# One in five of the low parts of the expert weights is formed on POOL

## The chip, the core and the metric

The kernel runs on one core of a Trainium2 chip. Its time is device microseconds (us) for one execution. Five engines work side by side, each through its own list of instructions in order: PE (TensorE) multiplies matrices, DVE (VectorE) and POOL (GpSimd) do elementwise work, ACT (ScalarE) does copies and functions, SP issues transfers. An instruction that waits for a semaphore holds up what stands behind it on the same engine.

## The reference

The computation is two transformer blocks on 256 tokens of width 1024, everything in fp32. The first has two layers; the second layer ends in a mixture of 8 experts, of which each token uses 2:

```
logits = xt @ router
top_v, top_i = top_k(logits, 2)
gates = one_hot(top_i) * softmax(top_v), summed over the two
out = sum over e of gates[:, e] * ((silu(xt @ w1[e]) * (xt @ w3[e])) @ w2[e])
```

Here w1[e] and w3[e] are 1024 x 1408 and w2[e] is 1408 x 1024. After it the second block (attention of two kinds, then a feed-forward layer) works on the result.

## The kernel before

**Split weights.** A matrix product in fp32 is made of three products in a faster format, fp32r. Each operand is cut in a high part h (the value rounded to fp32r) and a low part l (the value less h). `mm3` issues h·h, h·l and l·h into the same bank of PSUM. So each weight must be cut before PE can use it. The class `Stream` does that for all weights of the kernel, in the order of a list written beforehand (`plan`).

**One piece of weight.** `pump` issues a load from SP into a raw buffer as soon as one is free. A raw buffer holds 2048 elements in each of 128 partitions, which is two pieces of 1024 (or of 768, or in part of 512). `split` takes the next piece: ACT copies it, rounded, into the high tile, and DVE subtracts, `l = raw - h`, into the low tile. Both inputs of the subtraction lie in SBUF. When the last piece of a raw buffer has been cut, the buffer may be loaded again. `take` calls `split` first, so that the cutting of a piece is written out `ahead` pieces before the piece is used.

**Tiles for the parts.** High and low parts lie in a ring of four pairs of tiles (`wh`, `wl`). In the expert stage a fifth pair is there, a fixed tile named `more`, and `ahead` is 3 instead of 2. `turn` counts the pieces modulo five, and the pieces with turn 4 go to `more`. An expert has 36 pieces, all eight have 288, and 57 of these go to `more`.

**The expert stage.** For pairs of experts, the tokens that chose them are gathered by products with a 0/1 matrix (`gathered`, up to 128 tokens for each expert). Then for each expert, in three steps over the hidden width (512, 512 and 384), the products with w1 and w3 are made (`gemm`, tokens stationary), SiLU on ACT and the product of the two on DVE (tile `esil`), a transposition by PE, and a cut of the hidden values (`eh` on ACT, `el` on DVE) in `hidden_task`. The products with w2 follow, in two halves of 512 columns. `scatter_task` cuts the result (`yh`, `yl`), multiplies it by the 0/1 matrix and adds it to the sum with the gate as a factor (DVE, tile `X`). `drive` takes these tasks in turns, by a fixed rate. It reads no times, so the order of the instructions of this stage is fixed by the program alone.

**A second pass.** If more than 128 tokens chose one expert, a branch does the experts again for the rest, with a new `Stream` that has no `more` tile. The trace of before shows one pass.

**The planner's clocks.** Each engine is wrapped in a `Clock`, which adds up an assumed cost for every instruction written out. The stages before and after the experts are put in order by `timed`, which compares these clocks. The assumed cost is 200 + 2.0 ns for each element on POOL, and 160 + 1.04 ns for each element for a subtraction on DVE.

**POOL** does some clearing of tiles at the start, four copies of 128 x 128 in the second layer, and issues transfers. In the expert stage it has nothing to do.

In the trace nearly all instructions have line 47, where the wrapper calls the engine, so they are told apart by their tiles.

Of the kernel before, what the change touches and what calls it, by code (L numbers as in the profile page):

```python
# [153 lines left out]
def tile_net(ctx: ExitStack, tc: tile.TileContext, A, out):  # L154
# [4 lines left out]
    PE, ACT, DVE, POOL, SP = engines  # L159
# [33 lines left out]
    class Res:  # L193
# [3 lines left out]
        def __init__(self, pool, name, n, shape=(128, 512), dtype=F32):  # L197
            self.args = (list(shape), dtype)
            self.pool, self.name, self.n, self.free = pool, name, n, n
# [76 lines left out]
    class Pool:  # L276
# [7 lines left out]
        def give(self):  # L284
            self.free += 1
# [17 lines left out]
    class Stream:  # L303
        def __init__(self, base):
            self.base = base
            self.ahead, self.phase, self.ends = 2, 0, []
            self.more, self.turn = [], 0
            self.plan, self.loaded, self.subs = [], [], []
            self.at_load = self.at_split = self.at_take = 0
            self.limit = 1 << 30  # L310
# [38 lines left out]
        def split(self, ahead):  # L349
            self.pump()  # L350
            while self.at_split <= self.at_take + ahead and self.at_split < len(self.subs):
                v, n, c, give, phase = self.subs[self.at_split]
                if phase > self.phase:
                    return
                self.turn = (self.turn + 1) % (4 + len(self.more))
                if self.turn < 4:
                    h, l = (wsp.tile([128, 1024], F32R, name=x, tag=x) for x in ("wh", "wl"))
                else:
                    h, l = self.more[self.turn - 4]
                h, l = (x[:, :n * c].rearrange("p (k c) -> p k c", c=c) for x in (h, l))  # L360
                ACT.copy(out=h, in_=v)
                DVE.tensor_sub(out=l, in0=v, in1=h)
                self.subs[self.at_split] = (n, h, l)
                if give is not None:
                    give()
                self.at_split += 1
                self.pump()
# [8 lines left out]
    ws = Stream([main_raw])  # L376
# [59 lines left out]
    def drive(main, live, pend, rate=1.0, most=7, bg=None, bgn=1, drain=True):  # L436

        credit = owed = 0.0
        while True:
            if main is not None:  # L440
                try:
                    next(main)
                except StopIteration:
                    main = None
            older = list(live)
            credit = min(credit + rate, 2.0)
            while pend and credit >= 1 and len(live) < most:
                credit -= 1
                t = pend.pop(0)
                try:  # L450
                    next(t)
                    live.append(t)
                except StopIteration:
                    pass
            for t in older[::-1]:
                try:
                    next(t)
                except StopIteration:
                    live.remove(t)
            if bg is not None:  # L460
                owed = owed % 1 + (bgn[0] if isinstance(bgn, list) else bgn)
                for _ in range(int(owed) if main is not None else 1000):
                    try:
                        if next(bg):
                            break
                    except StopIteration:
                        bg = None
                        break
            if main is None and not live and not pend and bg is None:
                return  # L470
# [65 lines left out]
    h = const.tile([128, 4, D], F32, name="h")  # L536
# [1299 lines left out]
    with ExitStack() as ph:  # L1836
# [55 lines left out]
        ws.more.append(one.tile([128, 2, 1024], F32R, name="more").rearrange("p a b -> a p b"))  # L1892
        ws.turn = 0
        ws.ahead = 2 + len(ws.more)
        live = []

        def gate_task():
# [174 lines left out]
        with tc.If(over[0] > 128):  # L2072
            far = one.tile([128, 2, 8], F32, name="far")
            DVE.tensor_scalar(far, pos, 128.0, None, op0=OP.subtract)
            state = Clock.save(engines)
            again = Stream([])
            again.plan = ws.plan[moe_start:moe_end]
            keep, ws = ws, again
            drive(experts(far), live, [])
            ws = keep  # L2080
            Clock.back(engines, state)
        moe_pools.clear()
        ws.more = []
        ws.ahead, ws.turn = 2, 0
        ws.phase += 1
    wider.close()
# [522 lines left out]
```

## Time and profile before

| | |
|---|---|
| time, median of 3 runs | 1757.12 us (1753.77 to 1758.67) |
| time of the profiled execution | 1753.33 us |
| its span, first to last instruction | 1751.5 us |
| busy PE / DVE / ACT / POOL | 94% / 69% / 50% / 5% of the span |
| expert stage | some 415 us, from 885 to 1300 us of the span |

The profile gives the busy time of each engine and can be asked for a stretch of time, for the instructions on a tile, for the waits between engines and for a list in order of time. Ends of matmuls are modelled, so that PE counts as busy nearly everywhere when it has work in its pipe.

### The profile page before, as it was taken

The page shows a single profiled execution, that of the slowest core. Times are in us where ns is not written, and L with a number is a line of the kernel's source. Part 1 is how long each engine was busy: PE and PEld are TensorE (multiplying, and loading weights), DVE is VectorE, ACT ScalarE, POOL GpSimd, SP SyncE. Part 2 cuts the span into 40 slices and gives each one's busy share as a digit, 9 for nine tenths or more (in the row PEclk, how much of TensorE's full clock was granted, in tenths as well). Part 3 has the DMA queues.
Part 4 walks back from the last instruction along what each step waited for, and adds up shares of the span by engine and source line. Part 5 has one row for each costly group of instructions (what it writes and reads, how often), then busy time and mean ns, then how long its engine had stood idle before and what let it go on. Part 6 is the DMA issues. An engine that isn't in the chain of part 4 may idle for free. (4 is left out here: it accounts for less than half of the span.)

```text
span 1751.5 us, 23864 instructions
## 1 busy us (share of the span) xinstructions
PE 1654.4 (94%) x9260; PEld 1380.6 (79%) x9260; DVE 1208.4 (69%) x1847; ACT 875.2 (50%) x1320; POOL 80.6 (5%) x157
## 2 busy tenths in 40 slices
PE   5999999999999997997899999999989999989998
PEld 5878778877777776776688888887869889778897
DVE  3445555768665567678789888988985576675555
ACT  4334444321322225355477777777755556554443
POOL 1220000121011000000000000000000000000000
PEclk9999999999999998999999999999999999999999
DMA  9863322576567322223269899898956434345552
GB/s 287 288 215 95 109 60 85 198 210 215 173 217 238 123 73 93 70 79 121 84 223 338 316 361 340 294 337 307 353 182 189 137 109 145 120 158 185 177 177 86
DMA packets 187305, 331.31 MB, mean 189 GB/s; under 512 B 8174, under 2 KB 68992, under 8 KB 187184
## 3 DMA queue, kind: packets, MB, share of 16 engines
q1 hardware_dynamic: 172384, 279.73, 47.0%
q0 software_dynamic: 14800, 49.97, 8.9%
q8 instruction: 75, 1.23, 0.3%
q14 instruction: 46, 0.38, 0.1%
HBM read 328.59 MB, written 1.07 MB: 188 GB/s over the span
## 5 line engine op out<-in xcount | busy, mean ns | idle before, releaser
L47 DVE TENSOR_TENSOR wl<-raw,wh 128x1024 fp32r<-128x1024 f32 (+3 forms) x495 | 551.2, 1142 | 182.4 <-ACT wh L47 181.1
L47 ACT CAST wh<-raw 128x1024 fp32r<-128x1024 f32 (+3 forms) x495 | 473.1, 988 | 233.1 <-PE bank L47 220.6
L47 PE MATMUL bank<-aT,wh 128*128 128x512 f32 (+1 forms) x960 | 288.1, 383 | 1.7 <-DVE aT L47 1.6
L47 PEld LDWEIGHTS bank<-aT,wh 128*128 128x128 f32 x960 | 174.2, 188 | 41.9 <-issue 3.5
L47 PE MATMUL bank<-wh,aT 128*128 128x512 f32 (+2 forms) x640 | 193.3, 371 | 4.4 <-DVE aT L47 3.2
L47 PE MATMUL bank<-aT,wl 128*128 128x512 f32 (+1 forms) x480 | 182.6, 380 | 0.0
L47 PEld LDWEIGHTS bank<-wh,aT 128*128 128x128 f32 x640 | 118.0, 190 | 23.7 <-issue 6.0
L47 DVE SCALAR_TENSOR_TENSOR acc<-araw,sT,acc 128x1024 f32<-128x1024 f32 x70 | 88.2, 1281 | 47.1 <-DMA araw<-in_ada_w_dram 46.9
L47 PE MATMUL bank<-wl,aT 128*128 128x512 f32 (+2 forms) x320 | 116.5, 364 | 2.2 <-DVE wl L47 2.2
L47 PE MATMUL bank<-wl,gh 128*128 128x512 f32 (+1 forms) x306 | 115.7, 378 | 2.4 <-DVE wl L47 2.4
L47 PE MATMUL bank<-wh,gh 128*128 128x512 f32 (+1 forms) x306 | 116.7, 381 | 0.0
L47 PE MATMUL bank<-wh,gl 128*128 128x512 f32 (+1 forms) x306 | 115.7, 378 | 0.0
L47 PEld LDWEIGHTS bank<-aT,wl 128*128 128x128 f32 x480 | 90.1, 188 | 18.9
L47 PE MATMUL bank<-zT,wh 128*128 128x256 f32 x512 | 93.7, 285 | 0.0
L47 PEld LDWEIGHTS bank<-zT,wh 128*128 128x128 f32 x512 | 80.3, 190 | 0.5
L47 PE MATMUL bank<-zT,wl 128*128 128x256 f32 x256 | 72.6, 284 | 0.0
L47 PE MATMUL bank<-wh,xT 128*128 128x384 f32 (+2 forms) x256 | 69.7, 347 | 2.5 <-ACT wh L47 2.5
L47 PE MATMUL bank<-wh,hidl 128*128 128x512 f32 x176 | 69.9, 397 | 0.9 <-DVE hidl L47 0.9
L47 PE MATMUL bank<-wh,hidh 128*128 128x512 f32 x176 | 70.2, 399 | 0.0
L47 PE MATMUL bank<-wl,hidh 128*128 128x512 f32 x176 | 69.9, 397 | 0.1
L47 PEld LDWEIGHTS bank<-wl,aT 128*128 128x128 f32 x320 | 61.1, 191 | 9.6 <-DVE wl L47 3.5
L47 PEld LDWEIGHTS bank<-wl,gh 128*128 128x128 f32 x306 | 57.7, 188 | 12.9 <-DVE wl L47 3.9
(413 smaller groups left out, 3056.3 us busy)
## 6 DMA issues: line engine op xcount, KB each, us to landing
raw<-in_moe_w_dram SPq DMA_DIRECT2D x96, 1024.0 KB, 7.5
araw<-in_ada_w_dram POOLq DMA_DIRECT2D x80, 512.0 KB, 5.0
raw<-in_moe_w_dram SPq DMA_DIRECT2D x48, 768.0 KB, 5.7
raw<-in_w_ff_dram SPq DMA_DIRECT2D x32, 1024.0 KB, 5.4
raw<-in_ffn_w_dram SPq DMA_DIRECT2D x30, 1024.0 KB, 6.4
raw<-in_ev_w_in_dram SPq DMA_DIRECT2D x48, 256.0 KB, 4.4
raw<-in_w_in_dram SPq DMA_DIRECT2D x10, 1024.0 KB, 5.1
raw<-in_w_in_dram SPq DMA_DIRECT2D x12, 768.0 KB, 4.4
```

The costliest lines, as they stand in the source:

```text
L47: r = fn(*args, **kw)
```

## The change

`Stream` gets a flag `aside`. Where it is set and the piece goes to the fifth pair (turn 4, the tile `more`), the subtraction is issued on POOL instead of DVE. The flag is set for the expert stage and cleared after it. It is set for the stream of the second pass too.

```diff
@@ class Stream, __init__
             self.more, self.turn = [], 0
+            self.aside = False
@@ class Stream, split
                 ACT.copy(out=h, in_=v)
-                DVE.tensor_sub(out=l, in0=v, in1=h)
+                (POOL if self.aside and self.turn == 4 else DVE).tensor_sub(out=l, in0=v, in1=h)
                 self.subs[self.at_split] = (n, h, l)
@@ before the expert stage
         ws.turn = 0
         ws.ahead = 2 + len(ws.more)
+        ws.aside = True
@@ second pass, and after the stage
             again = Stream([])
+            again.aside = True
...
-        ws.more = []
+        ws.more, ws.aside = [], False
```

## Rows read from the trace of the kernel before

**Rows 1.** Page, head: span, then busy us and instructions of each engine

```profile
span 1751.5 us, 23864 instructions
PE 1654.4 (94%) x9260; PEld 1380.6 (79%) x9260; DVE 1208.4 (69%) x1847; ACT 875.2 (50%) x1320; POOL 80.6 (5%) x157
```

**Rows 2.** Busy us by stretch, expert stage: length, engines with counts, PEclk, DMA share, GB/s

```profile
885.00:1300.00 415.00, 404.80 (x1907) 334.90 (x1907) 374.71 (x412) 314.57 (x384) 0.00 (x0) 1.00 0.89 314
```

**Rows 3.** The same stretch, instructions on tile more alone: PE, PEld, DVE, ACT

```profile
885.00:1300.00 415.00, 82.26 (x330) 60.37 (x330) 64.71 (x57) 56.13 (x57) 1.00 0.89 314
```

**Rows 4.** Waits in the expert stage, PE: us in total, times, longest

```profile
PE bank L47 <- DVE el L47: 5.1, 8, 0.7
PE bank L47 <- DVE wl L47: 3.2, 4, 1.3
PE bank L47 <- DVE yl L47: 0.7, 3, 0.2
```

**Rows 5.** Waits in the expert stage, DVE, and SP's queue of loads

```profile
DVE el L47 <- ACT eh L47: 17.3, 14, 1.4
DVE wl L47 <- ACT wh L47: 14.1, 25, 1.4
...
SPq L47 <- DVE more L47: 85.9, 29, 14.0
```

**Rows 6.** Groups by shape, expert stage: the low parts in more; busy us, mean ns, idle before

```profile
L47 DVE TENSOR_TENSOR more<-raw,more 128x1024 fp32r<-128x1024 f32 x41 | 50.0, 1220 | 3.5 <-ACT more L47 3.2
L47 DVE TENSOR_TENSOR more<-raw,more 128x768 fp32r<-128x768 f32 x14 | 13.3, 952 | 0.1
L47 DVE TENSOR_TENSOR more<-raw,more 128x512 fp32r<-128x512 f32 x2 | 1.4, 682 | 0.0
```

**Rows 7.** Groups, expert stage: DVE operations with one input in PSUM

```profile
L47 DVE SCALAR_TENSOR_TENSOR X<-bank,gt,X 128x512 f32<-128x512 f32 x24 | 17.8, 743 | 0.0
L47 DVE TENSOR_TENSOR el<-bank,eh 128x512 fp32r<-128x512 f32 (+1 forms) x24 | 15.5, 644 | 17.5 <-ACT eh L47 17.3
L47 DVE TENSOR_TENSOR esil<-bank,esil 128x512 f32<-128x512 f32 (+1 forms) x24 | 15.3, 639 | 0.0
L47 DVE TENSOR_TENSOR yl<-bank,yh 128x512 fp32r<-128x512 f32 x14 | 9.6, 686 | 3.4 <-ACT yh L47 3.4
```

**Rows 8.** Timeline, POOL: start us, us, instruction, count; its copies

```profile
8.17 0.18 POOL L47 COPY ones<-ones 1x1 f32<-1x1 f32 x1
715.79 0.28 POOL L47 COPY P<-P 128x128 f32<-128x128 f32 x1 [127.24 <-DVE xr L47]
...
717.94 1.23 POOL L47 COPY P<-P 128x128 f32<-128x128 f32 x1 [0.24 <-DVE P L47]
```

**Rows 9.** Timeline, DVE, around these copies

```profile
714.69 0.36 DVE L47 TENSOR_TENSOR sw<-xr,rt 128x64 f32<-128x64 f32 x2
...
715.82 0.48 DVE L47 TENSOR_TENSOR sw<-xr,rt 128x64 f32<-128x64 f32 x2
...
717.79 1.22 DVE L47 TENSOR_TENSOR wl<-raw,wh 128x1024 fp32r<-128x1024 f32 x1
```

**Rows 10.** Timeline, DVE, expert stage: low parts one behind the other

```profile
1103.68 4.80 DVE L47 TENSOR_TENSOR wl<-raw,wh 128x1024 fp32r<-128x1024 f32 x4
...
1111.27 3.49 DVE L47 TENSOR_TENSOR wl<-raw,wh 128x1024 fp32r<-128x1024 f32 x3
1114.68 1.22 DVE L47 TENSOR_TENSOR more<-raw,more 128x1024 fp32r<-128x1024 f32 x1
```

**Rows 11.** Timeline, ACT and PE: high part of one more piece, its first use

```profile
1112.97 1.05 ACT L47 CAST more<-raw 128x1024 fp32r<-128x1024 f32 x1 [0.34 <-PE bank L47]
...
1118.82 0.63 PE L47 MATMUL bank<-more,gh 128*128 128x512 f32 x2
```

**Rows 12.** Timeline, POOL: first transfer that it issues after the experts

```profile
1315.70 0.54 POOL L47 DMA_DIRECT2D dm<-in_dil_mask_dram  x1 [477.67 <-DVEq L2072]
```

**Rows 13.** Busy us by stretch, attention of the second block (columns of rows 2, with POOL)

```profile
1320.00:1530.00 210.00, 198.59 (x1372) 182.19 (x1371) 132.43 (x246) 122.95 (x230) 0.54 (x1) 0.98 0.42 137
```

## The prediction

> **What bounds the kernel now.** I read the head of the page first: PE is busy for 1654.4 of 1751.5 us, DVE for 1208.4, POOL for 80.6 [rows 1]. The change touches the expert stage alone, so the next view is the busy time of that stretch. There PE is busy for 404.8 of 415 us at a full granted clock, and DVE for 374.7, which is 90% and leaves it 40.3 us idle [rows 2]. The reader should see that there are two engines near their limit here, and PE is the one that sets the end. The third view, the waits, says how much DVE costs PE now: 5.1 us for `el`, 3.2 for `wl` and 0.7 for `yl`, together 9.0 us [rows 4]. That is the most that relief of DVE can give in this stage, 0.5% of the kernel. The 40.3 us of DVE are also not free time of one kind: 17.3 us are waits of `el` for ACT and 14.1 us waits of `wl` for ACT [rows 5]. These stand in DVE's list wherever the data comes late.
>
> **What goes from DVE.** 57 subtractions (41 of 1024 elements, 14 of 768, 2 of 512) [rows 6], 64.7 us busy [rows 3]. DVE keeps 374.7 - 64.7 = 310.0 us.
>
> **What POOL gets.** The trace has no subtraction on POOL. Its nearest rows are copies: one element takes 0.18 us, 128 elements take 0.28 us where nothing is in the way [rows 8]. That is 0.10 us for 127 more elements, some 0.8 ns for one operand of one element. Two operands, read one after the other, would be 0.18 + 2 x 1024 x 0.8 ns = 1.8 us for a piece of 1024; read at once, as a lower end, 1.0 us. POOL has nothing else in this stage [rows 2], so 57 x 1.8 = 103 us of its own time cost nothing by themselves.
>
> **What POOL takes from DVE.** This is the term that decides. The fourth copy on POOL starts 0.15 us after DVE has started a low part (717.79, 1.22 us) and takes 1.23 us instead of 0.28; it ends 0.16 us after DVE ends at 719.01 [rows 8, 9]. So POOL's read stood still while DVE subtracted one SBUF tile from another. The other direction shows too, weakly: the same pair of small DVE operations takes 0.36 us without a copy beside it, and 0.48 us at 715.82, where POOL had begun its first copy at 715.79 [rows 8, 9]. 0.12 us for 128 elements read is 0.94 ns for each. A subtraction on POOL reads two operands, so it would hold DVE's two-input work for 2 x 1024 x 0.94 ns = 1.92 us (1.44 us for 768, 0.96 for 512). Over all: 41 x 1.92 + 14 x 1.44 + 2 x 0.96 = 100.8 us. The lower end is 0, since one pair of operations is thin evidence; the upper end is what POOL's whole instructions would come to, 103 us by the copies, so nearly the same. I take 100.8.
>
> [...]
>
> Not all of DVE's work is shut out. Operations with one operand in PSUM ran 17.8 + 15.5 + 15.3 + 9.6 = 58.2 us [rows 7], 19% of the 310.0 that stay. If the same share of the held time is filled with them, 19 us are hidden; all of the 58.2 would be the upper end, none the lower.
>
> **The sum.** DVE's work and held time: 310.0 + 100.8 - 19 = 391.8 us, 17.1 us more than now. With the 40.3 us of waits kept as they are, the stage takes 432 us instead of 415: +17 us. With nothing hidden it is 310.0 + 100.8 + 40.3 = 451, +36 us. With all the waits used up by the held time it is 391.8, less than the 415 that PE needs, and nothing is lost. The value that I take is +15, a little under the middle one, because a few of the 14.1 us of waits of `wl` [rows 5] would go where POOL holds DVE anyway.
>
> **What is covered.** POOL's piece may come later than DVE's did. ACT ends one high part at 1114.02 and PE first uses that piece at 1118.82, 4.8 us later [rows 11]; DVE had finished it by 1115.90 [rows 10]. With one DVE operation ahead of it (1.22) and its own 1.8 to 1.9 us, POOL takes 3.1 us, so PE doesn't wait. If this cover is gone, the price is the third rival's. Raw buffers come free later by the same 1.2 us; 29 loads wait for a `more` low part now, up to 14.0 us [rows 5], since they are queued long before they are needed, and the transfers are 89% busy [rows 2], so I cost this at nothing. Behind the 57 subtractions POOL's list has the transfers for the second block; the first is issued at 1315.70 [rows 12], after the stage, and stays there. In the second pass no tile `more` exists, so turn 4 never comes and the flag does nothing.
>
> The planner's clocks count 2248 ns on POOL instead of 1225 on DVE for a piece. `drive` reads no clocks, so the expert stage keeps its order. The stage behind it is ordered by clocks that start from other values, and could be put in another order: PE has 210.0 - 198.6 = 11.4 us idle there [rows 13], so I bound this by 11 us to either side and take 0.
>
> The profiled execution took 1753.33 us, 1.8 more than its span and 3.8 below the median of 1757.12. From its own time the sum gives 1768; put on the median it is 1772 us. That is the forecast.
>
> **Rivals.** *First, DVE is not held, and is only relieved.* Then the 9.0 us of PE's waits go at most: 1748, or 1753 if the waits on `el` stay (5.1), whose own wait for ACT (17.3 us) [rows 5] is not DVE's work. For it: only one pair of operations shows DVE held. Against: the fourth copy shows that the two engines do meet. It decides from the point where a low part on DVE keeps its 1.22 us beside POOL.
>
> *Second, DVE is held, but where it had nothing to do.* The 40.3 us idle and the 58.2 us of PSUM operations together nearly equal 100.8, so a lucky order loses nothing: 1757, with 5 us to either side. Against: the waits are short (1.4 us at most [rows 5]) beside 1.92.
>
> *Third, POOL is starved.* DVE's low parts stand one behind the other, 3.49 us for three and 4.80 for four [rows 10]. If POOL gets in only between such trains, its piece comes 3.5 + 1.9 = 5.4 or 4.8 + 1.9 = 6.7 us after ACT, 0.6 or 1.9 us past the cover of 4.8. 57 times that is 34 to 108 us; the middle is 71 and the time 1828. For it: the fourth copy waited out its whole DVE instruction. Against: the trains are broken by PSUM operations, and get shorter by every fifth piece.
>
> *Fourth, nothing happens*, because POOL's share is too small to be seen anywhere: 1757. Against it stands 64.7 us of work that moves.
>
> **How the numbers follow.** 0.3%, 5.3 us, is about what a measurement of this kernel can tell from no change. The forecast gets 0.53; its own range is 0 to +36, of which I put 0.44 above +5.3 and 0.09 within. The first rival gets 0.18 (0.12 faster, 0.06 within), the second 0.14 (0.10 within, 0.04 faster by the relief), the third 0.12, all slower, the fourth 0.03. Faster 0.16, same 0.28, slower 0.56. The range goes from 1746, just under the first rival, to 1835, which takes in the middle of the third; what lies beyond is less than 1 in 10. The forecast's own range is 1757 to 1793.
>
> **What would show it.** In the changed kernel's groups, the low parts `wl` of 1024 elements on DVE should have a mean well over 1.22 us, or idle time before them put down to POOL or to nothing; the mean tells which price holds: 100.8 us over the 231 low parts that stay on DVE (288 pieces less 57) is 0.44 us more on each. POOL should have 57 subtractions of 1.8 us or more, up to 3.1 where one waits for DVE. The stage from the first to the last `more` piece should be longer by the whole difference of the two times, and PE's waits for `wl` should grow from 3.2 us to well over 10. If the mean of `wl` stays at 1.22, the first rival is right; if PE waits for POOL on `more` at most turns, the third; if the difference is found after 1320, the planner's order did it. A time under 1752 or over 1793 makes the forecast wrong.

## The result, and the profile after

The changed kernel takes 1774.91 us (median of 4 runs, 1771.85 to 1776.31), beside 1757.45 us for the kernel before: slower by 17.5 us, a ratio of 1.011 with a 95% interval of 1.0094 to 1.0126. The forecast was 1772 and a range of 1746 to 1835. The profiled execution took 1773.64 us. Times below are medians of fast executions; one execution of the kernel with half pieces took 3249.70 us, was marked slow, and is left out of its median.

The head of the page shows where the work went. DVE has 57 instructions fewer than in [rows 1] and is busy for 17 us more; POOL has 57 more and 143 us more.

```profile
span 1771.9 us, 23915 instructions
...
PE 1659.7 (94%) x9260; PEld 1378.6 (78%) x9260; DVE 1225.3 (69%) x1790; ACT 875.5 (49%) x1320; POOL 223.2 (13%) x214
```

The expert stage now runs to some 1320 us of the span. Its busy times (PE, PEld, DVE, ACT, POOL, then clock, share and rate of the transfers) are the answer to [rows 2]:

```profile
885.00:1320.00 435.00, 412.24 (x1903) 334.88 (x1902) 390.26 (x354) 313.97 (x383) 142.38 (x57) 0.99 0.86 300
```

DVE lost 57 low parts, 64.7 us of work, and is still busy for 390.3 us instead of 374.7 (in a stage that is 20 us longer). The low parts that it kept have grown longer. First the kernel before, the groups by shape over the same stage, then the kernel after (busy us, mean ns of one, idle before):

```profile
L47 DVE TENSOR_TENSOR wl<-raw,wh 128x1024 fp32r<-128x1024 f32 x164 | 195.3, 1219 | 14.9 <-ACT wh L47 14.1
...
L47 DVE TENSOR_TENSOR wl<-raw,wh 128x768 fp32r<-128x768 f32 x50 | 45.7, 952 | 0.2
...
L47 DVE TENSOR_TENSOR wl<-raw,wh 128x512 fp32r<-128x512 f32 x13 | 8.9, 682 | 0.0
```

```profile
L47 DVE TENSOR_TENSOR wl<-raw,wh 128x1024 fp32r<-128x1024 f32 x163 | 249.0, 1561 | 28.6 <-ACT wh L47 28.3
L47 DVE TENSOR_TENSOR wl<-raw,wh 128x768 fp32r<-128x768 f32 x50 | 59.9, 1237 | 1.9 <-PE bank L47 1.0 <-ACT wh L47 0.7
L47 DVE SCALAR_TENSOR_TENSOR X<-bank,gt,X 128x512 f32<-128x512 f32 x24 | 17.8, 741 | 0.0
L47 DVE TENSOR_TENSOR el<-bank,eh 128x512 fp32r<-128x512 f32 x16 | 11.0, 687 | 7.8 <-ACT eh L47 7.8
L47 DVE TENSOR_TENSOR esil<-bank,esil 128x512 f32<-128x512 f32 x16 | 10.9, 680 | 1.7 <-PE bank L47 1.7
L47 DVE TENSOR_TENSOR wl<-raw,wh 128x512 fp32r<-128x512 f32 x13 | 10.2, 782 | 0.0
L47 DVE TENSOR_TENSOR yl<-bank,yh 128x512 fp32r<-128x512 f32 x14 | 9.6, 682 | 4.0 <-ACT yh L47 4.0
```

The operations that read two tiles of SBUF grew (1219 to 1561 ns, 952 to 1237). Those with one operand in PSUM did not: `X` is at 741 where [rows 7] had 743, `yl` at 682 where it had 686. POOL's new groups:

```profile
L47 POOL TENSOR_TENSOR more<-raw,more 128x1024 fp32r<-128x1024 f32 x41 | 109.9, 2681 | 263.8 <-ACT more L47 259.1 <-PE bank L47 4.8
...
L47 POOL TENSOR_TENSOR more<-raw,more 128x768 fp32r<-128x768 f32 x14 | 29.9, 2134 | 66.1 <-ACT more L47 66.1
```

Single instructions show the hold. The timeline of POOL, and that of DVE at two of its pieces:

```profile
1002.88 2.45 POOL L47 TENSOR_TENSOR more<-raw,more 128x1024 fp32r<-128x1024 f32 x1 [8.28 <-ACT more L47]
...
1125.07 2.83 POOL L47 TENSOR_TENSOR more<-raw,more 128x1024 fp32r<-128x1024 f32 x1 [3.37 <-ACT more L47]
```

```profile
1002.99 0.75 DVE L47 SCALAR_TENSOR_TENSOR X<-bank,gt,X 128x512 f32<-128x512 f32 x1
1003.65 2.77 DVE L47 TENSOR_TENSOR wl<-raw,wh 128x1024 fp32r<-128x1024 f32 x1
...
1125.57 3.41 DVE L47 TENSOR_TENSOR wl<-raw,wh 128x1024 fp32r<-128x1024 f32 x1
```

The `X` operation at 1002.99 lies wholly inside POOL's instruction and takes its usual 0.75 us. The low part behind it starts at 1003.65, and ends at 1006.42, 1.09 us after POOL's end at 1005.33. The one at 1125.57 ends at 1128.98, 1.08 us after POOL's end at 1127.90. Both had almost all of their own 1.22 us still to do when POOL was finished. It is so throughout the stage: 39 low parts of 1024 elements start while an instruction of POOL runs, and all 39 end 1.08 to 1.09 us after it.

The waits of PE, answering to [rows 4], in the stage:

```profile
PE bank L47 <- DVE wl L47: 12.5, 16, 3.0
...
PE bank L47 <- DVE el L47: 3.5, 6, 0.8
PE bank L47 <- POOL more L47: 3.4, 6, 0.8
```

With 0.7 us for `yl` these are 20.1 us, where the waits of [rows 4] came to 9.0. The 11 us between them are about half of what the stage is longer. Most of the rest stands in PE's busy time up to POOL's first transfer behind the stage (423.2 us after 414.6), where the ends of matmuls are modelled; up to 3.4 us of it is the clock's (below).

Behind the stage nothing changed. POOL's first transfer for the second block, 1315.70 in [rows 12], is issued at 1336.62, 20.9 us later. From there to the end of the span it is 435.3 us, and it was 435.8 (first the kernel after, then before):

```profile
1336.62:1771.90 435.28, 410.00 (x2645) 369.53 (x2643) 263.37 (x418) 225.84 (x360) 4.28 (x8) 0.98 0.45 149
```

```profile
1315.70:1751.50 435.80, 411.13 (x2645) 371.13 (x2643) 263.28 (x418) 225.93 (x360) 4.24 (x8) 0.97 0.45 149
```

### The profile page after: what moved, and what is told of

It is laid out like the page before. It is cut to its first block, busy times and chain, and to the rows that moved or that the text cites. A ratio compares the mean times of both kernels' runs of the same rounds, so it can differ in the third digit from the quotient of the medians.

```text
span 1771.9 us, 23915 instructions
## 1 busy us (share of the span) xinstructions
PE 1659.7 (94%) x9260; PEld 1378.6 (78%) x9260; DVE 1225.3 (69%) x1790; ACT 875.5 (49%) x1320; POOL 223.2 (13%) x214
## 3 DMA queue, kind: packets, MB, share of 16 engines
q8 instruction: 75, 1.23, 0.3%
HBM read 328.59 MB, written 1.07 MB: 186 GB/s over the span
## 5 line engine op out<-in xcount | busy, mean ns | idle before, releaser
L47 DVE TENSOR_TENSOR wl<-raw,wh 128x1024 fp32r<-128x1024 f32 (+3 forms) x495 | 621.4, 1286 | 198.3 <-ACT wh L47 196.5
L47 POOL TENSOR_TENSOR more<-raw,more 128x1024 fp32r<-128x1024 f32 (+2 forms) x57 | 142.6, 2501 | 339.2 <-ACT more L47 334.5
L47 POOL DMA_DIRECT2D araw<-in_ada_w_dram x80 | 42.4, 531 | 420.7 <-DVE acc L47 308.0
```

Of the source, the lines that this page charges most:

```text
L47: r = fn(*args, **kw)
```

## Is it the hold, or POOL's lateness?

Four kernels take the change apart. Theory H is that POOL's reads hold DVE; its rival L, that PE waits for POOL's piece. Differences are of medians, with the kernel before timed beside them on the same chip, and the ratio's interval in brackets.

**Relief alone.** The 57 low parts are not formed.

```diff
-                (POOL if self.aside and self.turn == 4 else DVE).tensor_sub(out=l, in0=v, in1=h)
+                if self.aside and self.turn == 4:
+                    l = h
+                else:
+                    DVE.tensor_sub(out=l, in0=v, in1=h)
```

> The low part of the 57 pieces in the tile more is not formed at all; PE multiplies by the high part in its place, so PE's work is the same. Theory H (POOL's reads of SBUF hold DVE's subtractions) and rival L (the piece from POOL only comes too late for PE) both expect what relief alone is worth: DVE busy 310 us in the stage, low parts on DVE at 1.22 us, PE's waits for DVE (9.0 us before) nearly gone, time 1748 to 1753 us.

Measured: 1744.91 beside 1754.94 us, 10.0 us faster (0.9922 to 0.995). Low parts on DVE had a mean of 1221 ns, as expected; the time is some 3 us under the range that was expected. Relief is worth about the 9.0 us that the waits of PE came to, or a little more (8.8 to 13.7 by the interval). DVE's busy time up to the first transfer behind the stage fell by 55.9 us (384.2 to 328.3), less than the 64.7 us of the instructions that are gone: neighbours on DVE overlap a little in the records, as `X` and the low part behind it do above (0.09 us).

**The hold alone.** DVE does all it did, and POOL does its part once more.

```diff
+                DVE.tensor_sub(out=l, in0=v, in1=h)
+                if self.aside and self.turn == 4:
+                    POOL.tensor_sub(out=spot[:, :n * c].rearrange("p (k c) -> p k c", c=c), in0=v, in1=h)
...
+    spot = h[:, 3, :]
```

> DVE forms all low parts as before, and POOL forms those of the 57 pieces once more into a place that nobody reads. H: DVE keeps its 374.7 us and is held by some 80 us on top, the low parts go from 1.22 to about 1.5 us or more, time 1797 to 1837 us. L: nobody waits for POOL's result, so 1757 us, low parts at 1.22 us.

Measured: 1825.21 us, 70.3 us slower (1.0383 to 1.042), in the range of H. Nobody reads what POOL writes here. DVE's groups:

```profile
L47 DVE TENSOR_TENSOR wl<-raw,wh 128x1024 fp32r<-128x1024 f32 (+2 forms) x229 | 327.8, 1469 | 7.3 <-ACT wh L47 6.8
L47 DVE TENSOR_TENSOR more<-raw,more 128x1024 fp32r<-128x1024 f32 (+2 forms) x57 | 84.1, 1476 | 3.8 <-ACT more L47 3.5
```

The two groups together take 411.9 us; before they took 250.2 and 64.7. That is 97 us of hold, and L has no place for a loss of 70. Another way in which POOL's reads could cost time, that ACT waits for POOL before it writes the next piece, came to 2.8 us in the whole run. A part of the 70 may be slower matmuls: the granted clock of the stage was 0.97, and 1.00 before.

**Lateness without reading.** POOL clears the low tile four times.

```diff
+                if self.aside and self.turn == 4:
+                    for _ in range(4):
+                        POOL.memset(f(l), 0.0)
+                else:
+                    DVE.tensor_sub(out=l, in0=v, in1=h)
```

> In place of the subtraction POOL clears the low tile four times (some 0.9 us each, 3.7 us in all, the time that ACT's copy and POOL's subtraction take together), reading nothing; the low parts of the 57 pieces are zero. H: nothing is held, low parts on DVE at 1.22 us, time within 3 us of the run in which these parts are not formed, 1748 to 1756. L: PE waits for the tile more as in the changed kernel, some 1775 us.

Measured: 1748.81 us, 6.1 us faster (0.995 to 0.9976), in the range of H, though 3.9 us over the run of relief alone, where the expectation had at most 3. POOL is busy for longer than in the changed kernel, and DVE's low parts keep their length:

```profile
L47 POOL MEMSET more<- 128x1024 f32 x164 | 156.9, 957 | 194.9 <-PE bank L47 164.1 <-DVE gy L47 23.7
```

```profile
L47 DVE TENSOR_TENSOR wl<-raw,wh 128x1024 fp32r<-128x1024 f32 x165 | 196.8, 1220 | 45.5 <-ACT wh L47 45.2
```

The clearing doesn't wait for ACT, so it starts earlier than the subtraction did, but it ends about as late: 2.2 us after ACT's cast of the piece in the median, 2.5 in the changed kernel. So a piece that is ready at about the same moment lost nothing against the kernel before when POOL didn't read.

**One operand.** POOL copies the raw value.

```diff
+                if self.aside and self.turn == 4:
+                    POOL.tensor_copy(out=l, in_=v)
+                else:
+                    DVE.tensor_sub(out=l, in0=v, in1=h)
```

> POOL copies the raw value into the low tile instead of subtracting: one operand read instead of two. H: half the hold, so the 1024-wide low parts on DVE have a mean of about 1.39 us (1.22 without POOL, 1.56 in the changed kernel), time about halfway between the run without these parts and the changed kernel, 1758 to 1765 us. L: POOL's piece is ready sooner than DVE's was, so as without these parts, 1748 to 1753 us, low parts at 1.22 us.

Measured: 1751.42 us, 3.5 us faster (0.9966 to 0.9994); low parts on DVE at 1305 ns. The mean grew by 84 ns, a quarter of the changed kernel's 342 and not half, so H missed both the mean and the time. The time lies in the range of L, but L has no place for low parts that grow, and the run is 6.5 us over the one of relief alone.

The trace tells why the mean grew so little. Each hold lasts to the end of POOL's instruction, as with the subtraction: of 27 low parts of 1024 elements that start while a copy runs, 23 end 1.07 to 1.08 us after it. (The copy from 917.17 to 919.04 us holds the low part that starts at 918.05; it takes 2.06 us.) But the holds are fewer and shorter: 23 low parts of 1024 elements are lengthened, by 0.62 us in the mean, where the changed kernel has 39, by 1.44 us. A copy that meets nothing takes 1.05 us instead of 2.40, and it starts some 1.3 us before ACT's cast ends, since it needn't wait for it. How much each of the two makes, the run doesn't tell.

So H stands: what loses the time is POOL reading while DVE subtracts. The held low parts of the changed kernel end 1.08 to 1.09 us after POOL's instruction (1024 elements, 39 of 39), and beside clearing, where POOL only writes, they stay at 1220 ns.

## Does time follow the sum of the holds?

The sum of DVE's work and held time gave the right answer in the prediction. The next runs ask whether that was the mechanism (theory O), or whether each hold costs where it makes a low part late (S).

**One in ten.** Every second of the 57 goes back to DVE.

```diff
+                self.count += self.turn == 4
+                far = self.aside and self.turn == 4 and self.count % 2 == 0
+                (POOL if far else DVE).tensor_sub(out=l, in0=v, in1=h)
```

> Every second of the 57 subtractions goes back to DVE, so 28 are on POOL. The hold is taken as shown now; open is whether time follows the sum of DVE's work and held time (theory O) or each long hold that makes a low part late (rival S, steps). Relief is half of the 11 us that the run without these parts gave, the hold half of what the changed kernel lost against it (29 us of 18 + 11). O and S both expect some 9 us over the kernel before, 1763 to 1767 us; a threshold below which DVE's idle time takes the holds up would give 1755 to 1758.

Measured: 1766.65 beside 1754.5 us, 12.2 us slower (1.0053 to 1.008). With 28 pieces on POOL, DVE's idle time did not take the holds up.

**Half of each piece.** POOL takes the right half of the columns, DVE the left.

```diff
+                if self.aside and self.turn == 4:
+                    m = c // 2
+                    POOL.tensor_sub(out=l[:, :, m:], in0=v[:, :, m:], in1=h[:, :, m:])
+                    DVE.tensor_sub(out=l[:, :, :m], in0=v[:, :, :m], in1=h[:, :, :m])
```

> POOL forms the right half of the columns of the 57 low parts and DVE the left half. O: DVE is relieved of 57 x (1.13 - 0.65) = 27 us instead of 65 and held for about half as long as in the changed kernel, 40 us of 80, so DVE's work and held time are 13 us more than before, against 16 there: about 1770 us. S: the holds are 1.3 us instead of 2.4 and mostly taken up, 1755 to 1762 us.

Measured: 1760.54 beside 1754.5 us, 6.0 us slower (1.002 to 1.0056), in the range of S and well under O's. What O builds on came out as expected: DVE's busy time up to the first transfer behind the stage rose by 12.2 us (384.2 to 396.3). The time rose by half of that. The run had 57 short holds, and lost less than the one with 28 long ones.

**Quarters.** The same subtraction as four instructions on POOL.

```diff
+                if self.aside and self.turn == 4:
+                    m = c // 4
+                    for j in range(4):
+                        POOL.tensor_sub(out=l[:, :, j * m:(j + 1) * m], in0=v[:, :, j * m:(j + 1) * m],
+                                        in1=h[:, :, j * m:(j + 1) * m])
```

> POOL's subtraction is written as four of a quarter of the columns each, so that DVE may get in between them. O: the held time stays or grows by the three more starts of some 0.2 us each (57 x 0.6 = 34 us at most), time 1775 to 1800 us. S: each hold is some 0.7 us instead of 2.4 and DVE's low parts come less late, time below 1766 us.

Measured: 1797.25 us, 42.8 us slower (1.0232 to 1.027). The time is in O's range for another reason than O's. DVE is held less than in the changed kernel: its 229 low parts take 286.3 us, where they took 320.3 there and 250.2 before. Now it is POOL that is late:

```profile
PEld bank L47 <- POOL more L47: 48.6, 28, 3.6
...
PE bank L47 <- POOL more L47: 37.5, 26, 3.2
```

A quarter takes 1.06 us in the mean and 0.72 for 256 elements where it meets nothing, because POOL and DVE took turns here: in the timeline from 1013.25 us on four quarters take 5.30 us, and from 1014.54 us on three low parts of 1024 elements take 5.09 us, where three took 3.49 in [rows 10]. So the last quarter ends 4.2 us after ACT's cast in the median of the 57 pieces, where the whole subtraction ended after 2.5. PE's first use comes 4.1 us after the cast in the median, so about half of the pieces come too late. (The cover of 4.8 us in [rows 11] is that of one piece; in the kernel before it goes from 1.2 to 8.1 us, 4.0 in the median.) This has the effect of the prediction's third rival, lateness past the cover, but not its mechanism: POOL isn't kept out by a train of low parts, it waits four times. The granted clock of the stage was 0.98, and 1.00 before, so a part of the loss may be slower matmuls.

**Halves.** The same with `range(2)` and `c // 2`.

> POOL's subtraction as two of half the columns each. Theory S (time is lost where one hold is longer than the low part's cover, and where POOL's piece comes later than its cover of some 4.8 us): two holds of at most 1.3 us instead of one of 2.4, POOL's piece ready 2.6 us of its own and one or two waits of 1.1 us after ACT, so within the cover: 1752 to 1764 us. Theory O (the sum of DVE's work and held time): the same hold and 57 more starts, 1774 to 1785 us.

Measured: 1772.78 beside 1754.16 us, 18.6 us slower (1.0099 to 1.0129), just under O's range and outside S's. Both costs are there: low parts at 1473 ns for 1024 elements, and 14.6 us of waits of PE for POOL. Cutting POOL's instruction in two gained nothing (18.6 us lost, and 17.5 with one).

**Quarters that nobody reads.** As quarters, into `spot`, with `l = h`.

> POOL subtracts in quarters as in the run before, but into a place that nobody reads, and PE takes the high part in place of the 57 low parts, so that PE waits for POOL nowhere. S and the reading that PE's waits for POOL's late piece (37.5 us in the run with quarters) made that run slow: 1744 to 1752 us, for DVE is held for only some 36 us and relieved of 65. If the holds themselves made it slow: above 1765 us.

Measured: 1763.98 us, 9.8 us slower (1.0037 to 1.0063). Neither reading had it. PE waits for no piece of POOL here, so of the 42.8 us some 33 came with POOL's lateness. But DVE's busy time in the stage (375.0 us up to the first transfer behind it, 384.2 before) is below that of the kernel before, and the run is slower all the same. The sum alone doesn't make the time. This run by itself doesn't show that the holds do: POOL's quarters read the high part too, and ACT waited 14.9 us for POOL before it could cast the next piece into `more`. The half pieces above are free of that and speak against O as well.

**A ring of six.** A sixth pair of tiles, taken from the spare raw buffers, in the kernel before and in the changed one.

```diff
-            spare.pieces.extend(pieces)
+            spare.pieces.extend([two[0][:, 0], two[0][:, 1]])
+            sixth.append(two[1][:, 0])
...
+        ws.more.append(sixth[0].rearrange("p (a b) -> p a b", a=2).rearrange("p a b -> a p b"))
```

> The kernel before with a sixth pair of tiles in the ring (and ahead 4), taken from the raw buffers, 6 instead of 8; all low parts on DVE. It is the measure for the next run. PE's 9.0 us of waits for DVE shrink with more cover: 1748 to 1757 us; if six raw buffers are too few for the loads, above 1760.

> The changed kernel with the sixth pair of tiles; POOL has 48 low parts, one in six, and every piece 1.4 us more cover. S: holds of up to 2.4 us are mostly covered, less than 6 us over the run with the ring of six alone. O: 48/57 of the loss stays, 14 to 18 us over that run, because DVE's work and held time are what they are.

Measured: 1758.97 us with all low parts on DVE, 4.8 us slower than before (1.0019 to 1.0037), which neither part of its expectation had, and 1768.28 us with one in six on POOL. The 48 pieces cost 9.3 us, 0.19 each, where 57 cost 17.5, 0.31 each. That is between S (under 6) and O (14 to 18). DVE's busy time up to the first transfer behind the stage rose by 20.5 us over the ring of six alone (383.6 to 404.1), more than the 17.1 of the changed kernel, and cost less. So more cover takes away about a third of the loss; with some 3 us of noise on each of the two differences, how much is not sharp.

**Where the loss falls.** ACT's cast of each piece in `more` marks the progress. The start of the n-th cast (us of the span), and how far it lies behind the kernel before (last column: the same for the run of relief alone):

```
 n    before    after   behind  relief alone
 1    886.20   886.27    +0.1      +1.3
 4    907.95   911.36    +3.4      +0.6
 7    927.24   932.08    +4.8      -0.3
25   1061.56  1068.70    +7.1      -2.2
29   1087.54  1097.57   +10.0      -3.2
36   1139.80  1152.50   +12.7      -4.0
42   1182.01  1195.25   +13.2      -4.0
43   1190.06  1204.75   +14.7      -4.9
55   1278.83  1294.88   +16.1      -5.8
57   1294.80  1316.66   +21.9      -7.2
```

The kernel falls behind in steps: 3.4 us in the first 22 us, 5.8 us over the last two pieces, and for the rest mostly at pieces that belong to w2 (7, 28, 36, 43) or stand right behind it (29), while it keeps its distance over most of w1 and w3. The 19 pieces of w2 take 12.9 of the 21.9 us, the 38 of w1 and w3 the other 9.0. Relief pays at some of the same places. In the kernel before, DVE is busy for 19.5 of 20 us from 1130 on, in the products with w2, and for 18.2 of 20 from 1106 on, in those with w1 and w3.

The last step isn't the hold alone. From 1309.9 to 1316.7 us of the span TensorE's granted clock was 0.50, and it fell while PE waited 3.0 us for a `wl`, until 1310.9; in the kernel before it was 1.00 from 885 to 1313 us. A matmul of 512 columns took 0.63 us there instead of 0.40, so of these 6.8 us up to 3.4 are the clock's, an estimate from the clock of 0.50.

So one more run put POOL only where DVE has time over (lines that set the counter to 0 are left out here):

```diff
+                self.count += 1
+                far = self.aside and self.turn == 4 and self.count > 36 and (self.count - 1) % 36 < 24
+                (POOL if far else DVE).tensor_sub(out=l, in0=v, in1=h)
```

> POOL forms only those of the 57 low parts that belong to the products with w1 and w3 of experts 2 to 8: 34 of them; the others (all of the first expert, and those of w2) go back to DVE. Reading W (where): the changed kernel falls behind in steps, nearly all in the products with w2, at the start and at the end of the stage, and keeps its distance through w1 and w3, where DVE has time over; so these 34 cost little, 0 to 5 us over the kernel before, 1754 to 1760 us. Reading C (count): each held low part costs the same, 34/57 of 19 us, 1765 to 1768 us.

Measured: 1762.48 beside 1754.8 us, 7.7 us slower (1.0028 to 1.0054), between the two. These 34 pieces cost 0.23 us each; the other 23 of the changed kernel's 57 cost 9.8 us, 0.43 each. So the place seems to matter, by a factor of about two; the interval of this run alone leaves 0.14 to 0.28 for the 34, and the 0.43 carries the noise of both runs and the clock of the last step. No place that was tried made the change pay. No run that forms every low part was faster than the kernel before.

## Why the prediction was right

The number was right, within 3 us, and so was the deciding cause: DVE is held by POOL's reads. That the number came so close is partly luck, as the terms show.

**What goes from DVE** went, 57 instructions and 64.7 us of them. DVE's busy time is relieved of less, 55.9 us by the run of relief alone. Its worth, the upper end of the first rival, was put at 9.0 us from PE's waits on DVE, and that run gave 10.0.

**What POOL gets** was too small: 1.8 us for a piece of 1024. The shortest in the trace of after take 2.39 us (1024), 1.84 (768) and 1.29 (512), some 2.2 ns for each element, where the copies of [rows 8] had made it 1.6. It cost nothing in itself, as said: PE waits for POOL for 3.4 us only, and the longest instruction on POOL, 3.46 us, is its 2.40 and one operation of DVE.

**What POOL takes from DVE** was the term that decided, and its direction came from one lengthened copy on POOL and one lengthened pair on DVE [rows 8, 9]. Both were real. Its size was off in two places. The hold was priced at 1.92 us for a piece, the reading time; the traces show it lasting to the end of POOL's instruction, which takes 2.4 us. And only 19 us of it were to be hidden, by operations with one operand in PSUM. That these are not held no row of before shows; the changed kernel does, where five `X` operations that start beside an instruction of POOL take 0.73 to 0.75 us each. No run shows the 19 us as such: POOL was busy for 142.4 us, and DVE's low parts grew by 70.1 (320.3 less 250.2), so half of POOL's time lengthened no low part. Net, 81.8 us of hold were forecast, and DVE's busy time is 73.0 us over that of relief alone (401.3 less 328.3). So the hold came out 8.8 us smaller than forecast, and the relief 8.8 us smaller (55.9 for 64.7). That the two cancel is luck; it is why the result on DVE, 391.8 us forecast and 390.3 measured, is right.

**The sum** kept DVE's 40.3 us of waits as they were, and they were 44.7 after (435 less 390.3). The mean of the 1024-wide low parts grew by 0.34 us; 0.44 was forecast over all. What the sum hid is the mechanism by which the hold becomes time. It took DVE's busy time to set the length of the stage. The runs side by side (us against the kernel before, DVE's busy time up to the first transfer behind the stage; the ring of six against its own measure):

| run | DVE busy | time |
|---|---|---|
| changed kernel | +17.1 | +17.5 |
| one in ten | +3.2 | +12.2 |
| half of each piece | +12.2 | +6.0 |
| w1 and w3 only | +11.1 | +7.7 |
| ring of six | +20.5 | +9.3 |
| the hold alone | +99.2 | +70.3 |

The two agree for the changed kernel, and for no other; so this step of the prediction was right in its result and not in its reason. What fits the runs is that time is lost where a hold makes a low part late for PE: more cover and shorter holds cost less at the same busy time or more. But S as it was put isn't a rule either: quarters, halves, the quarters that nobody reads and the ring of six came out above its ranges. That most is lost where DVE has no time over is likely, and not shown beyond the noise.

**What was costed at nothing** stayed so: the loads (SP's waits for a piece in `more` went from 85.9 us [rows 5] to 57.9, and no engine waited for a load in this stage), POOL's transfers, and the planner's order, for the second block took 435.3 us after 435.8.

What stays open: what one hold costs at a given place. It was 0.19 us with a ring of six, 0.23 in the products with w1 and w3, 0.43 elsewhere, and 28 of them on a DVE that keeps more of its work cost as much as 0.44 each. These are net costs, the relief within them; no run here gives a rule that holds for all of them.

## What to carry to other kernels

Before work goes from DVE to POOL, look in the trace for any instruction on POOL that ran beside DVE, and compare it with its like alone: one copy of 1.23 instead of 0.28 us told the direction here. In the changed kernel a subtraction of two SBUF tiles of 1024 elements took POOL twice DVE's time (2.40 us for 1.22), and each of the 39 low parts of 1024 elements that start beside it ends only after it, by 1.08 to 1.09 us. So the price is not POOL's time but what waits behind DVE. Moving less of it, or moving it elsewhere, only made the loss smaller; cutting it in smaller parts on POOL made it no smaller (halves) or larger (quarters). And a sum that gives the right time may do so by luck: try it on a second kernel where its terms stand otherwise.

## What the runs showed of the hardware that was not expected

Who got in next was not the same each time. In the changed kernel the longest wait of a whole piece on POOL was about one low part (3.46 us against 2.40), and a piece cut in four waited again and again, so that its quarters took 1.06 us in the mean. But with all low parts on DVE (the hold alone) one subtraction on POOL took 6.05 us from 955.57: three low parts one behind the other passed in it at their usual 1.21 us before the next one, at 959.95, was held. So POOL was kept out by a train of low parts there, as the third rival had it; it was rare (this one and one of 4.88 us for 768 elements, among 57).

A copy with one operand on POOL held a low part to its own end as a subtraction does (23 of 27 end 1.07 to 1.08 us after it); it is shorter (1.05 us alone), and the low parts grew by 84 ns in the mean. Clearing lengthened them not at all (1220 ns, and 1219 before).
